# Output projection of a hybrid decoder layer: sixteen token blocks of plain products, or eight block pairs of Strassen's seven products

## The chip, the cores and the metric

One core of one Trainium2 chip runs the whole layer in one launch. The time is device microseconds (us) of that core; smaller is better. Engines: PE = TensorE (matrix products into PSUM), DVE = VectorE, ACT = ScalarE, POOL = GpSimd, SP = SyncE (here it only issues DMAs).

## The reference

Sequence 2048, width 1024, one layer, float32. Only the end is touched by the change:

```python
h = rms_norm(x, ln_g)
proj = h @ w_in                                  # then two head groups
y_mla = mla_group(...) * silu(g_mla)             # 8 heads, causal softmax attention, (2048, 512)
y_hg  = hgrn2_group(...) * silu(g_hg)            # gated linear recurrence, (2048, 512)
x = x + concatenate([y_mla, y_hg], -1) @ w_out   # w_out is (1024, 1024)
return rms_norm(x, final_norm_g)
```

## The kernel before, in words

Float32 operands are split into two fp32r parts, `hi` (a cast, on ACT) and `lo` (the value minus `hi`, on DVE or POOL). A product is three matmuls, hi·hi, hi·lo, lo·hi, all summed in PSUM (`mm3`, L67 to L70).

The program has three stages. Up to about 700 us it does the input projection and the recurrence. Then comes **attention**: 8 heads of 8 steps, 64 steps in all, each of 256 queries. Step n runs stage B of (head, j) together with stage A of the next step. Stage A: scores in three matmuls (L881 to L883), DVE moves them out of PSUM with the running minimum (L886, L890), ACT takes the exponential (L895) into an `sn` row tile (four buffers). Stage B: PE transposes the `sn` tiles (L929), ACT casts the result to `ph` (L932), DVE makes `pl` (L933), PE applies them to the values (L947, L948), POOL scales the gate (L914), and `finish` (L953 to L962) multiplies by the gate on POOL (L960) and stores 64 rows of `y` into `y_d` in DRAM (L962). Between these, pieces of the next head's work are placed (keys, values, queries; POOL makes their `lo` at L814, L829, L842).

The **output projection** stands behind. `load_wout` (L974 to L990) runs at step 60 (`WOUT = 4` steps into the last head): four loads of 1 MB of `w_out` (L979), eight casts of 128x1024 on ACT (L984), eight subtractions (L985, the first on DVE, seven on POOL). The loop of L1040 to L1080 then goes over 16 blocks of 128 tokens: load the block of `y` transposed (L1047), cast on ACT (L1048), `lo` on DVE (L1049), load `x` (L1051); for each of two halves of 512 columns, 8 x 3 matmuls of 128x512 (`mm3`), DVE adds `x` (L1062), ACT squares and sums (L1063); POOL starts the sum (L1066), DVE multiplies by `final_norm_g` (L1067) and ends the sum (L1069), POOL takes the power (L1072), ACT scales one half (L1073), DVE the other (L1074), and SP stores (L1076 to L1079). The last block's second half is cut in two. That is 744 matmuls of 128x512 and 48 of 128x256.

A scheduler sets the order of each engine's instructions from the program; every engine then takes its own in that order and waits at each for what it needs. SP issues all DMAs in one order too. Matmuls of the output projection for early blocks are placed among the last steps of attention, where they fill PE's time.

Of the kernel before, what the change touches and what calls it, by code (L numbers as in the profile page):

```python
# [10 lines left out]
F32 = mybir.dt.float32  # L11
# [5 lines left out]
ALU = mybir.AluOpType  # L17
# [20 lines left out]
WOUT = 4  # L38
# [19 lines left out]
def hybrid_kernel(ctx: ExitStack, tc: tile.TileContext, x, x_t, positions, ln_g, w_in, q_a_norm_g, w_q_b,  # L58
# [719 lines left out]
    def prep(h):  # L778
# [52 lines left out]
        def query(c):  # L831
# [5 lines left out]
            qf = wk.tile([128, 512], F32, tag="qf", bufs=1, name="qf")  # L837
            V.tensor_tensor(qf, p, csT[:, sl], ALU.mult)
            qh = wk.tile([128, 512], F32R, tag="qh", bufs=2, name="qh")
            ql = wk.tile([128, 512], F32R, tag="ql", bufs=2, name="ql")  # L840
# [64 lines left out]
    def stage_b(h, j, ctx_, par):  # L905
# [44 lines left out]
        def finish():  # L950
# [6 lines left out]
            tmp = wk.tile([64, 256], F32, tag="oa", name="oa")  # L957
# [16 lines left out]
    def load_wout():  # L974
        p2r.close()
        wo = p2r.enter_context(tc.tile_pool(name="wo", bufs=1, side="right"))
        for k2 in range(KT // 2):
            wr = wk.tile([128, 2, D], F32, tag="vp", name="vp")
            DMA.dma_start(wr, w_out[k2 * 256:(k2 + 1) * 256, :].rearrange("(k p) n -> p k n", p=128))  # L979
            for j in range(2):  # L980
                k = 2 * k2 + j
                a = wo.tile([128, D], F32R, name=f"wo_hi{k}")
                b = wo.tile([128, D], F32R, name=f"wo_lo{k}")
                A.copy(a, wr[:, j])  # L984
                (V if k == 0 else G).tensor_tensor(b, wr[:, j], f32(a), ALU.subtract)  # L985
                w_hi.append(a)
                w_lo.append(b)
# [48 lines left out]


    p3 = ExitStack()
    op = p3.enter_context(tc.tile_pool(name="op", bufs=2, side="right"))
    fng = wk.tile([128, D], F32, tag="ks", bufs=1, name="ks")  # L1040
    DMA.dma_start(fng, final_norm_g.rearrange("(o n) -> o n", o=1).broadcast_to([128, D]))
    for b in range(NBLK):
        c, r0 = b // 4, b * 128
        t0 = (b % 4) * 128
        yh = op.tile([128, KT, 128], F32R, tag="yh", name="yh")
        yl = op.tile([128, KT, 128], F32R, tag="yl", name="yl")
        DMA.dma_start(f32(yl), y_d[c][:, t0:t0 + 128].rearrange("(k p) t -> p k t", p=128))  # L1047
        A.copy(yh, f32(yl))  # L1048
        V.tensor_tensor(yl, f32(yl), f32(yh), ALU.subtract)  # L1049
        xt = wk.tile([128, D], F32, tag="vp", name="vp")  # L1050
        DMA.dma_start(xt, x[r0:r0 + 128, :])  # L1051
        last = b == NBLK - 1
        cuts = (0, 512, 768, 1024) if last else (0, 512, 1024)
        ssq = small.tile([128, 3], F32, tag="ssq3", name="ssq3")
        ot = wk2.tile([128, D], F32, tag="sn", bufs=4, name="sn")
        r = None
        for i in range(len(cuts) - 1):
# [53 lines left out]
```

## Time and profile before

| | us |
|---|---|
| median of 3 runs (1418.79, 1419.00, 1421.24) | 1419.0 |
| the profiled execution's own time | 1418.87 |
| its span, first to last instruction | 1417.1 |
| PE busy | 1387.7 |
| DVE busy | 958.6 |
| ACT busy | 881.2 |
| POOL busy | 464.8 |

The span is divided among engines in the page's first part; an engine can be busy beside others, so the shares don't add up. The chain of waits follows back from the last instruction what released each instruction, so its shares do add up. A window gives each engine's busy time in a stretch.

### The profile page before, as it was taken

How to read it: one execution, taken by the hardware profiler on the slowest of the kernel's cores; microseconds unless marked ns; L12 is line 12 of the kernel's file. 1: busy time of each engine (PE TensorE's matmuls, PEld its weight loads, DVE VectorE, ACT ScalarE, POOL GpSimd, SP SyncE). 2: the span in 40 equal slices, each digit the busy share in tenths (PEclk: the TensorE clock that was granted, in tenths of full speed). 3: DMA queues.
4: the chain of work that ended last, by engine and by line, in shares of the span. 5: the costliest groups of instructions: out<-in, count | busy, mean ns of one | idle time of the engine just before them, and what ended most of it. 6: DMA issues, size and time to landing. Idle time of an engine off the chain costs nothing.

```text
span 1417.1 us, 25792 instructions
## 1 busy us (share of the span) xinstructions
PE 1387.7 (98%) x9258; PEld 1263.5 (89%) x9258; DVE 958.6 (68%) x2425; ACT 881.2 (62%) x1796; POOL 464.8 (33%) x635
## 2 busy tenths in 40 slices
PE   8999999999999999999899999999999999999998
PEld 7899879989899988998889898999999998888887
DVE  6547855595845845658388889898889889743333
ACT  6565575456862647355388778778777878732232
POOL 3123613083121622237252425233342525411010
PEclk9999999999999999999989999999999999999999
DMA  7211211215411112111630000100010103244442
GB/s 230 75 48 46 75 53 31 67 42 172 138 46 34 54 52 82 38 42 44 194 73 18 19 22 13 24 13 22 13 26 11 25 22 107 74 144 143 134 148 104
DMA packets 100576, 96.30 MB, mean 68 GB/s; under 512 B 31200, under 2 KB 88800, under 8 KB 100320
## 3 DMA queue, kind: packets, MB, share of 16 engines
q1 hardware_dynamic: 100448, 94.65, 22.7%
q8 instruction: 73, 1.20, 0.4%
q14 instruction: 55, 0.45, 0.1%
HBM read 68.41 MB, written 25.17 MB: 66 GB/s over the span
## 4 chain that ended last, share of the span: by engine, by line
PE 85%; DVE 5%; POOL 3%; ACT 2%; issue 2%; DMA 2%; SPq 0%; POOLq 0%; DVEq 0%; ACTq 0%
PE ps_mm L68 14%; PE ps_mm L69 14%; PE ps_mm L70 14%; PE ps_tp L929 8%; PE ps_a L948 5%; PE ps_a L947 4%; PE ps_mm L881 4%; PE ps_mm L883 4%; PE ps_mm L882 4%; PE ps_b L70 2%; PE ps_b L68 2%; PE ps_b L69 2%; PE ps_a L486 2%; PE ps_b L486 1%; POOL dd L468 1%
## 5 line engine op out<-in xcount | busy, mean ns | idle before, releaser
L68 PE MATMUL ps_mm<-w,hh 128*128 128x256 f32 (+3 forms) x896 | 268.3, 299 | 0.0
L69 PE MATMUL ps_mm<-w,hh 128*128 128x256 f32 (+3 forms) x896 | 263.9, 295 | 0.0
L70 PE MATMUL ps_mm<-w,hl 128*128 128x256 f32 (+3 forms) x896 | 263.0, 294 | 0.0
L933 DVE TENSOR_TENSOR pl<-ps_tp,ph 128x512 fp32r<-128x512 f32 (+1 forms) x288 | 184.6, 655 | 33.3 <-ACT ph L932 32.6
L932 ACT CAST ph<-ps_tp 128x512 fp32r<-128x512 f32 (+1 forms) x288 | 154.4, 565 | 60.2 <-PE ps_tp L929 46.7
L68 PEld LDWEIGHTS ps_mm<-w,hh 128*128 128x128 f32 x896 | 170.1, 190 | 0.7
L69 PEld LDWEIGHTS ps_mm<-w,hh 128*128 128x128 f32 x896 | 169.8, 189 | 0.4
L70 PEld LDWEIGHTS ps_mm<-w,hl 128*128 128x128 f32 x896 | 169.3, 189 | 0.1
L929 PE MATMUL ps_tp<-ident,sn 128*128 128x128 f32 x1088 | 167.9, 274 | 0.8 <-ACT sn L895 0.8
L895 ACT ACTIVATE sn<-sn,mx 128x128 f32<-128x128 f32 (+15 forms) x128 | 154.6, 1208 | 21.2 <-DVE mx L890 20.8
L947 PE MATMUL ps_a<-ph,vp 128*128 128x256 f32 x576 | 155.5, 290 | 0.0
L948 PE MATMUL ps_a<-pl,vp 128*128 128x256 f32 x576 | 147.1, 288 | 0.2 <-DVE pl L933 0.2
L468 POOL TENSOR_TENSOR dd<-G 128x512 f32<-128x512 f32 x80 | 92.8, 1164 | 142.9 <-DVE qd L481 106.9
L929 PEld LDWEIGHTS ps_tp<-ident,sn 128*128 128x128 f32 x1088 | 126.8, 140 | 8.8 <-ACT sn L895 1.3
L881 PE MATMUL ps_mm<-k_hi,qh 128*128 128x512 f32 (+3 forms) x320 | 130.8, 409 | 0.5 <-DVE mx L890 0.2
L886 DVE TENSOR_SCALAR_CACHE_REDUCE sn<-ps_mm,mx 128x512 f32<-128x512 f32 (+3 forms) x192 | 111.5, 581 | 10.9 <-PE ps_mm L883 8.8
L883 PE MATMUL ps_mm<-k_hi,ql 128*128 128x512 f32 (+3 forms) x320 | 116.5, 364 | 1.4 <-DVE ql L842 1.4
L882 PE MATMUL ps_mm<-k_lo,qh 128*128 128x512 f32 (+3 forms) x320 | 116.1, 363 | 0.0
L914 POOL TENSOR_SCALAR gp<-gate,ri 128x64 f32<-128x64 f32 x128 | 56.7, 445 | 180.9 <-DVE ri L897 159.7
L230 DVE SCALAR_TENSOR_TENSOR w<-wr,lng,w 128x256 fp32r<-128x256 f32 (+3 forms) x168 | 89.3, 574 | 39.4 <-ACT w L229 39.4
L948 PEld LDWEIGHTS ps_a<-pl,vp 128*128 128x128 f32 x576 | 109.0, 189 | 6.0 <-DVE pl L933 1.2
L947 PEld LDWEIGHTS ps_a<-ph,vp 128*128 128x128 f32 x576 | 108.9, 189 | 5.8 <-ACT ph L932 0.6
(275 smaller groups left out, 3348.5 us busy)
## 6 DMA issues: line engine op xcount, KB each, us to landing
wr<-in_w_in SPq DMA_DIRECT2D x68, 256.0 KB
yl<-y_d SPq DMA_DIRECT2D x16, 512.0 KB
vp<-in_x SPq DMA_DIRECT2D x16, 512.0 KB
out<-sn SPq DMA_DIRECT2D x15, 512.0 KB
xt<-in_x SPq DMA_DIRECT2D x8, 512.0 KB
xs<-in_x_t SPq DMA_DIRECT2D x8, 512.0 KB
y_d<-yt SPq DMA_DIRECT2D x16, 256.0 KB
gate<-gate_d SPq DMA_DIRECT2D x8, 512.0 KB
```

The lines of the kernel that those rows point to most:

```text
L68: PE.matmul(ps, l_hi, r_hi, start=start, stop=False)
L69: PE.matmul(ps, l_hi, r_lo, start=False, stop=False)
L70: PE.matmul(ps, l_lo, r_hi, start=False, stop=stop)
L881: PE.matmul(p[:, :w], qh[:, qs], kh[:, ks], start=True, stop=False)
L882: PE.matmul(p[:, :w], qh[:, qs], kl[:, ks], start=False, stop=False)
L883: PE.matmul(p[:, :w], ql[:, qs], kh[:, ks], start=False, stop=True)
L895: A.activation(sn[:, :nk], sn[:, :nk], AF.Exp, bias=mx[:, kc:kc + 1], scale=-1.0, accum_out=rs)
L929: PE.transpose(tp[:, o:o + 128], prow[i][:, (kb + u) * 128:(kb + u + 1) * 128], ident)
L932: A.copy(ph[:, :w], tp[:, :w])
L933: V.tensor_tensor(pl[:, :w], tp[:, :w], f32(ph[:, :w]), ALU.subtract)
L947: PE.matmul(dst, vv, ph[:, rng], start=st_, stop=False)
L948: PE.matmul(dst, vv, pl[:, rng], start=False, stop=en)
```

## The change

The output projection is computed by the Winograd form of Strassen's scheme. For a pair of 128-token blocks, `y` is split into four quadrants (token block by half of the 1024 inner values: a11, a12, a21, a22) and `w_out` into four of 512x512 (b11, b12, b21, b22). Seven products of 128x512 with an inner length of 512 take the place of eight, on sums of quadrants: s1 = a21 + a22, s2 = s1 - a11, s3 = a11 - a21, s4 = a12 - s2, and t1 = b12 - b11, t2 = b22 - t1, t3 = b22 - b12, t4 = b21 - t2 (the sign of t4 as the code has it). Partial sums stay in PSUM: bank a takes a11·b11, is copied to bank b by ACT (L1205), then also takes a12·b21; b takes s2·t2, is copied to bank c (L1210), then takes s3·t3 and a22·t4; c takes s4·b22; e takes s1·t1. Each product is 12 matmuls (`product`, L1166 to L1168). The last pair's seventh product is cut in two halves of 256 columns. Two more matmuls of 128x512 (L1154) start banks b and c.

The weight sums are made by `wout_sums` (L991 to L1023) in eight items (128 rows of each half of `w_out`, 256 columns of each half): two loads (L1004), four POOL subtractions of 128x256 (L1010 to L1013), two ACT casts (L1018, 128x1024 and 128x768), two POOL `lo` subtractions of the same shapes (L1019), four stores (L1021) into `w_d` in DRAM. That is 14 MB stored, and read back as seven sets of 2 MB (`wload`, L989): b11, t1, t2, b21, t3 from step 59 on (`WOUT = 3`), b22 and t4 in the last step, when pool `big` is closed. The written plan gives item i the steps 8 + 6i and on.

`pair_operands` loads a pair's `y` (L1064, 1 MB) and `x` (L1070, 1 MB), makes the sums s1 to s4 on DVE (L1082, 128x512) and splits seven operands (ACT cast L1074, DVE L1075, 128x512 each). `after` adds `x` (L1172, six of 128x512 a pair) and ends as before (L1181 to L1201).

```diff
-WOUT = 4
+WOUT = 3
...
-    def load_wout():
...
+    ORDER = (("a11", "b11", "a"), ("s1", "t1", "e"), ("s2", "t2", "b"), ("a12", "b21", "a"),
+             ("s3", "t3", "b"), ("s4", "b22", "c"), ("a22", "t4", "b"))
...
+        def sums():
+            w, t = o["w"], four()
+            o["t"] = t
+            G.tensor_tensor(t[:, 0], w[:, 1], w[:, 0], ALU.subtract)
+            G.tensor_tensor(t[:, 1], w[:, 3], t[:, 0], ALU.subtract)
+            G.tensor_tensor(w[:, 1], w[:, 3], w[:, 1], ALU.subtract)
+            G.tensor_tensor(t[:, 2], w[:, 2], t[:, 1], ALU.subtract)
+
+        def split(src, s0, n):
+            hi = four(F32R)
+            lo = src[:, :n].bitcast(F32R)
+            A.copy(hi[:, :n], src[:, :n])
+            G.tensor_tensor(lo, src[:, :n], f32(hi[:, :n]), ALU.subtract)
+            for i, t in enumerate((hi[:, :n], lo)):
+                DMA.dma_start(f32(w_d[:, s0:s0 + n, i, kk, ns]), f32(t))
...
+    for i in range(8):
+        for k, f in enumerate(wout_sums(i // 2, i % 2)):
+            pieces[8 + 6 * i + k] = [f]
...
+            side = [open_wout, early("b11")]
+        elif first > 0 and n < len(seq) - 1:
+            side = side + [early(name) for name in {1: ("t1",), 2: ("t2", "b21"), 3: ("t3",)}[first]]
+        elif n == len(seq) - 1:
+            side = [open_late] + pair_operands(0)[:4] + [late("b22"), late("t4")]
...
-    for b in range(NBLK):
...
+        def residual():
+            xt = wk2.tile([128, 2, D], F32, tag="sn", bufs=4, name="sn")
...
+            DMA.dma_start(xt, x[r0:r0 + 256, :].rearrange("(r p) n -> p r n", p=128))
...
+        def after(i):
+            if i == 0:
+                A.copy(acc["b"], acc["a"])
+            elif i == 1:
+                add(0, H1, acc["e"])
+                add(1, H1, acc["e"])
+            elif i == 2:
+                A.copy(acc["c"], acc["b"])
+            elif i == 3:
+                add(0, H0, acc["a"])
+                done(0, H0, True)
...
+    run(pair_operands(0)[4:])
+    for b in range(NBLK // 2):
+        merge(pair_products(b), pair_operands(b + 1) if b + 1 < NBLK // 2 else [])
```

Where the scheduler puts these can't be read from the diff. Three places matter. In the rows below, a row is one instruction (x2, x3: so many alike), and the brackets name the engines and DMA queues it waits for; line numbers of the kernel before are lower by two in attention.

**POOL in the first steps of attention, before** (`gp` is the gate, `oa` the finished values, `ql` the query's `lo`):

```order
L914 TENSOR_SCALAR gp<-gate,ri 128x64 [waits DMAHW4_49,DMAHW3_49,DMAHW5_49,DMAHW1_49,DMAHW6_49,DMAHW0_49,DVE_49]
L914 TENSOR_SCALAR gp<-gate,ri 128x64 [waits DVE_49] x3
L814 TENSOR_TENSOR vp<-vs,vp 128x4x64 [waits Activation_49]
L960 TENSOR_TENSOR oa<-oa,og 64x256 [waits DVE_49]
L842 TENSOR_TENSOR ql<-qf,qh 128x512 [waits PE_49,Activation_49]
L914 TENSOR_SCALAR gp<-gate,ri 128x64 [waits DVE_49,PE_49]
L814 TENSOR_TENSOR vp<-vs,vp 128x4x64 [waits Activation_49]
L960 TENSOR_TENSOR oa<-oa,og 64x256 [waits DVE_49]
```

**The same place in the change:**

```order
L1010 TENSOR_TENSOR ss<-ss 128x256 [waits DMAHW6_49]
L1011 TENSOR_TENSOR ss<-ss 128x256 [waits DMAHW7_49,Pool_49]
L1012 TENSOR_TENSOR ss<-ss 128x256
L916 TENSOR_SCALAR gp<-gate,ri 128x64 [waits DMAHW1_49,DVE_49]
L1013 TENSOR_TENSOR ss<-ss 128x256 [waits Pool_49]
L916 TENSOR_SCALAR gp<-gate,ri 128x64 [waits DVE_49] x2
L1019 TENSOR_TENSOR ss<-ss 128x1024 [waits Activation_49,Pool_49]
L916 TENSOR_SCALAR gp<-gate,ri 128x64 [waits DVE_49]
L816 TENSOR_TENSOR vp<-vs,vp 128x4x64 [waits Activation_49]
L962 TENSOR_TENSOR oa<-oa,og 64x256 [waits DVE_49]
```

The eight items' 48 POOL instructions (`ss`) stand in the rows that belong to steps 0 to 14, between the gates and the `lo` of the next head, and not at the steps of the written plan.

**DVE near the end of attention, before** (`pl` belongs to the last steps' stage B, L1062 is the first block's adding of `x`):

```order
L933 TENSOR_TENSOR pl<-ps_tp,ph 128x512 [waits PE_49,Activation_49] x2
L1062 TENSOR_TENSOR vp<-ps_mm,vp 128x512 [waits DMAHW4_49,DMAHW6_49,DMAHW2_49,DMAHW7_49,PE_49,Pool_49]
L933 TENSOR_TENSOR pl<-ps_tp,ph 128x512 [waits DVE_49,Activation_49]
L1067 TENSOR_TENSOR vp<-vp,ks 128x512 [waits Activation_49]
L933 TENSOR_TENSOR pl<-ps_tp,ph 128x384 [waits Activation_49]
L933 TENSOR_TENSOR pl<-ps_tp,ph 128x512 [waits Activation_49] x2
L1062 TENSOR_TENSOR vp<-ps_mm,vp 128x512 [waits PE_49]
L1069 SCALAR_TENSOR_TENSOR rx<-ssq_15799,rx 128x1 [waits Activation_49,Pool_49]
```

**DVE in the last step, in the change:**

```order
L935 TENSOR_TENSOR pl<-ps_tp,ph 128x512 [waits Activation_49]
L1172 TENSOR_TENSOR sn<-ps_mm,sn 128x512 [waits DMAHW1_49]
L1172 TENSOR_TENSOR sn<-ps_mm,sn 128x512
L935 TENSOR_TENSOR pl<-ps_tp,ph 128x512 [waits PE_49,Activation_49] x2
L935 TENSOR_TENSOR pl<-ps_tp,ph 128x512 [waits Activation_49] x2
L935 TENSOR_TENSOR pl<-ps_tp,ph 128x384 [waits Activation_49]
L1075 TENSOR_TENSOR pl<-vp,ph 128x512 [waits PE_49,Activation_49] x2
L961 TENSOR_TENSOR oa<-ps_a,oa 64x256 [waits DMAHW5_49,Activation_49]
L1172 TENSOR_TENSOR sn<-ps_mm,sn 128x512 [waits PE_49] x2
L1189 TENSOR_TENSOR sn<-sn,fng 128x512 [waits Activation_49]
L1172 TENSOR_TENSOR sn<-ps_tp,sn 128x512 [waits PE_49]
L1082 TENSOR_TENSOR ss<-vp 128x512 [waits DMAHW6_49]
```

The first two additions of `x` (L1172, out of bank e) now stand between two `pl` of the last step and wait for the DMA of pair 0's `x`; the sums and splits for pair 1 (from L1082) come in a row behind.

**SP in the last step, in the change** (`y_d` is stored by `finish`; L1070 loads `x` for pairs 0 to 3, the last L1064 loads `y` for pair 1):

```order
L964 DMA y_d_71<-oa 64x256 [waits DMAHW5_49,Pool_49]
L989 DMA b22s<-wd 128x4096 [waits DMAHW6_49,PE_49,Activation_49]
L989 DMA t4s<-wd 128x4096 [waits DMAHW7_49,Activation_49]
L964 DMA y_d_71<-oa 64x256 [waits DMAHW0_49,Pool_49]
L1070 DMA sn<-in_x 128x2x1024 [waits DMAHW1_49,PE_49,Activation_49]
L1070 DMA sn<-in_x 128x2x1024 [waits DMAHW2_49,PE_49,Activation_49]
L964 DMA y_d_72<-oa 64x256 [waits DMAHW3_49,Pool_49]
L1070 DMA sn<-in_x 128x2x1024 [waits DMAHW4_49,PE_49,Activation_49]
L1070 DMA sn<-in_x 128x2x1024 [waits DMAHW5_49,PE_49,Activation_49]
L1064 DMA vp<-y_d_69 128x8x256 [waits DMAHW6_49,PE_49]
```

Pair 0's `x` is issued behind the reloads of b22 and t4, and waits for PE, that is for the last transposes out of the `sn` tile that it takes over; pair 1's `y` is issued behind four loads of `x` and waits for the last application of the values on PE (`vp`).

## Rows read from the trace of the kernel before

**Rows 1.** The page's first part: busy us (share of span), instructions of each engine.

```profile
PE 1387.7 (98%) x9258; PEld 1263.5 (89%) x9258; DVE 958.6 (68%) x2425; ACT 881.2 (62%) x1796; POOL 464.8 (33%) x635
```

**Rows 2.** The page's fourth part: shares by engine of the chain that ended last.

```profile
PE 85%; DVE 5%; POOL 3%; ACT 2%; issue 2%; DMA 2%; SPq 0%; POOLq 0%; DVEq 0%; ACTq 0%
```

**Rows 3.** Windows: busy us of PE, PEld, DVE, ACT, POOL (instructions), clock, DMA share, GB/s.

```profile
720.00:845.00 125.00, 124.76 (x851) 113.69 (x850) 108.37 (x347) 99.85 (x210) 45.02 (x69) 1.00 0.08 19
1185.00:1206.00 21.00, 19.91 (x124) 16.52 (x123) 20.07 (x59) 20.28 (x35) 13.75 (x12) 1.00 0.48 149
1224.00:1411.00 187.00, 186.91 (x899) 157.23 (x896) 73.68 (x118) 59.73 (x117) 22.48 (x37) 1.00 0.39 128
```

**Rows 4.** Timeline of PE, first output-projection matmuls: start us, us, instruction.

```profile
1224.10 0.48 PE L68 MATMUL ps_mm<-wo_hi,yh 128*128 128x512 f32 x1
1224.64 0.40 PE L70 MATMUL ps_mm<-wo_hi,yl 128*128 128x512 f32 x1
1227.86 0.40 PE L69 MATMUL ps_mm<-wo_lo,yh 128*128 128x512 f32 x1
```

**Rows 5.** Timelines of PE and SP at the end of the span.

```profile
1409.31 0.28 PE L68 MATMUL ps_b<-wo_hi,yh 128*128 128x256 f32 x1
1410.63 0.28 PE L70 MATMUL ps_b<-wo_hi,yl 128*128 128x256 f32 x1
1413.95 0.38 SPq L1076 DMA_DIRECT2D out<-sn  x1
```

**Rows 6.** Groups of instructions by line and shape: busy us, mean ns, idle before.

```profile
L932 ACT CAST ph<-ps_tp 128x512 fp32r<-128x512 f32 x224 | 125.9, 589 | 56.2 <-PE ps_tp L929 43.3 <-PE ps_a L947 10.3
L1048 ACT CAST yh<-yl 128x1024 fp32r<-128x1024 f32 x16 | 16.8, 1050 | 10.4 <-DMA yl<-y_d 10.3
L1049 DVE TENSOR_TENSOR yl<-yl,yh 128x1024 fp32r<-128x1024 f32 x16 | 20.1, 1254 | 23.6 <-ACT yh L1048 23.6
L1062 DVE TENSOR_TENSOR vp<-ps_mm,vp 128x512 f32<-128x512 f32 x21 | 14.5, 688 | 24.4 <-PE ps_mm L70 23.1 <-DMA vp<-in_x 1.2
L1063 ACT ACTIVATE sn<-vp 128x512 f32<-128x512 f32 x31 | 19.6, 632 | 89.7 <-DVE vp L1062 85.7 <-PE ps_tp L929 4.0
L814 POOL TENSOR_TENSOR vp<-vs,vp 128x256 fp32r<-128x256 f32 x24 | 17.4, 737 | 21.8 <-ACT vp L813 21.8
L985 POOL TENSOR_TENSOR wo_lo<-vp,wo_hi 128x1024 fp32r<-128x1024 f32 x7 | 16.8, 2414 | 5.8 <-ACT wo_hi L984 5.8
```

**Rows 7.** Timeline of ACT in attention, around 1185 us.

```profile
1185.43 2.00 ACT L984 CAST wo_hi<-vp 128x1024 fp32r<-128x1024 f32 x2
1190.25 2.24 ACT L1048 CAST yh<-yl 128x1024 fp32r<-128x1024 f32 x2
```

**Rows 8.** Timeline of PE just behind it.

```profile
1193.68 1.20 PE L929 MATMUL ps_tp<-ident,sn 128*128 128x128 f32 x9 [0.76 <-ACT sn L895]
```

**Rows 9.** Timelines of SP and ACT: one weight load issued, and its first use.

```profile
1202.25 0.38 SPq L979 DMA_DIRECT2D vp<-in_w_out  x1
1207.88 2.00 ACT L984 CAST wo_hi<-vp 128x1024 fp32r<-128x1024 f32 x2
```

**Rows 10.** Timeline of POOL beside VectorE, around 1192 us.

```profile
1191.70 2.05 POOL L960 TENSOR_TENSOR oa<-oa,og 64x256 f32<-64x256 f32 x1
1193.36 1.47 DVE L1049 TENSOR_TENSOR yl<-yl,yh 128x1024 fp32r<-128x1024 f32 x1
```

**Rows 11.** Windows: a stretch with much DMA traffic.

```profile
1186.00:1190.00 4.00, 3.89 (x22) 3.03 (x21) 3.75 (x12) 3.95 (x8) 2.49 (x2) 1.00 0.95 260
```

**Rows 12.** Timeline of PE: an idle time ahead of attention.

```profile
703.95 0.55 PE L68 MATMUL ps_mm<-wv_hi,c_hi 128*128 128x256 f32 x1 [2.28 <-ACT gt L365]
```

**Rows 13.** Windows around it.

```profile
700.00:704.00 4.00, 1.72 (x12) 1.36 (x10) 1.12 (x3) 1.90 (x4) 0.27 (x1) 1.00 1.04 256
704.00:716.00 12.00, 7.75 (x22) 5.66 (x23) 10.84 (x19) 10.01 (x19) 10.53 (x10) 0.50 0.97 252
716.00:720.00 4.00, 4.00 (x23) 3.43 (x23) 2.89 (x13) 2.61 (x8) 2.56 (x4) 0.79 0.99 163
```

More of the change, by code (lines that the diff above doesn't have):

```diff
@@ L956, in finish @@
                 A.copy(gs[:, i * 128:(i + 1) * 128], gT[i * 64:(i + 1) * 64, 0:128])
[L957 removed]
+            tmp = wk.tile([64, 256], F32, tag="oa", bufs=3, name="oa")
             A.copy(tmp, av[64:128])
@@ new lines, in hybrid_kernel, with wload, wout_sums, four @@
+    wset = {}
+    ys = [{} for _ in range(NBLK // 2)]
+    o_pools = {}
+    SETS = ("b11", "t3", "b21", "b22", "t1", "t2", "t4")
+    w_d = dram.tile([128, 7, 2, 4, 512], F32R, name="wd")
+    def wload(pool, name):
+        wset[name] = pool.tile([128, 2, 4, 512], F32R, name=name + "s")
+        DMA.dma_start(f32(wset[name]), f32(w_d[:, SETS.index(name)]))
+    def wout_sums(kk, ch):
+        ns = slice(ch * 256, ch * 256 + 256)
+        o = {}
+        def four(dtype=F32):
+            return fin.tile([128, 4, 256], dtype, tag="ss", bufs=3, name="ss")
+        def load():
+            o["w"] = four()
+            for g in range(2):
+                r0 = g * 512 + kk * 128
+                DMA.dma_start(o["w"][:, 2 * g:2 * g + 2],
+                              w_out[r0:r0 + 128, :].rearrange("p (c n) -> p c n", c=2)[:, :, ns])
+        def sums():
[12 more added lines that the diff above has]
+                DMA.dma_start(f32(w_d[:, s0:s0 + n, i, kk, ns]), f32(t))
+        return [load, sums, lambda: split(o["w"], 0, 4), lambda: split(o["t"], 4, 3)]
@@ new lines, in late, with operand @@
+    def late(name):
+        return lambda: wload(o_pools["ln"], name)
+    ln = ExitStack()
+    def operand(name):
+        if name in ("a11", "s1"):
+            if "ks" not in o_pools:
+                o_pools["ks"] = wk.tile([128, 2, 2, 4, 128], F32R, tag="ks", bufs=1, name="ks")
+            t = o_pools["ks"][:, ("a11", "s1").index(name)]
+        elif name == "s2":
+            t = o_pools["ln"].tile([128, 2, 4, 128], F32R, tag=name, name=name)
+        elif name in ("s3", "s4"):
+            t = wk2.tile([128, 2, 4, 128], F32R, tag="gate", name="gate")
+        else:
+            return (wk2.tile([128, 4, 128], F32R, tag="ph", bufs=3, name="ph"),
+                    wk2.tile([128, 4, 128], F32R, tag="pl", bufs=3, name="pl"))
+        return t[:, 0], t[:, 1]
```

170 lines of the change are left out of this document (110 added, 60 removed).

## The prediction, made before the changed kernel had run

> **What bounds the kernel now.** I read the page's busy times first, to find the fullest engine: PE is busy 1387.7 of 1417.1 us, 98%, and no other engine is over 68% [rows 1]. The chain of waits then says whether that fullness sets the end: PE holds 85% of it, DVE 5% [rows 2]. Shares are averages, so I read windows by stage. In the output projection PE is busy 186.91 of 187 us while DVE has 73.7 and ACT 59.7 [rows 3]: it is bound by PE alone, and work taken from PE comes off the time if the others keep up. In attention PE is busy too (124.76 of 125), but there DVE has 108.4, ACT 99.9 and POOL 45.0 [rows 3]: PE's lead is thin, and what is added on ACT or POOL must be checked. The profiled execution took 1418.87 us, 1.8 over its span and 0.1 under the median of the runs, so the sum below is made against 1418.9. About 0.2% (2.8 us) is what a measurement of this kernel can tell from no change.
>
> **1. Products: -21.7.** Fourteen matmuls of 128x512 start in 1227.86 - 1224.64 = 3.22 us, 0.23 each [rows 4]; eleven of 128x256 in 1410.63 - 1409.31 = 1.32, 0.12 each [rows 5]. Before: 744 of the wide and 48 of the narrow. Now: 8 pairs x 7 x 12 = 672, of which the last 12 are cut into 24 halves, so 660 wide, 24 narrow, and two wide ones that start banks b and c. Saved: 84 x 0.23 + 24 x 0.12 - 2 x 0.23 = 21.7. PE is gapless there, so all of it comes off.
>
> **2. `load_wout` goes: -1.** Its casts lie on ACT in pairs of 2.00 us, and two of L1048 in 2.24 [rows 7]. Behind these PE waits 0.76 for the exponential [rows 8]; the stretch loses 1.1 of 21 [rows 3]. Pair 0's splits come into the same last steps, so I take 1 between 0 and -1.1, nearer the row's loss, as they are single casts of about 0.59 [rows 6].
>
> **3. Weight sums in steps 0 to 14: +2.** The order puts all eight items there. Each costs POOL four subtractions of 0.74, one of 2.41, and one of three quarters of that, 1.81 [rows 6]: 7.2, times eight 57.5. POOL goes from 45.0 of 125 to about 102, 82%. ACT gets 1.05 + 0.79 per item, 14.7 in all, and goes from 99.9 to 114.6, 92%; DVE stays at 108.4. PE's queue waits in order for POOL's `ql` and `gp` and ACT's `ph`. Lower end 0, as this stretch loses 0.24 now. Upper end: where ACT is at 97% and DVE at 96%, PE lost 1.1 of 21 [rows 3], over 125 us that is 6.5. ACT stays below that, so 2. The 18 MB that the items load and store in this stretch meet a DMA share of 0.08 [rows 3]; the stores wait for POOL on SP, and behind them stand the next heads' loads and `y`'s stores, which have steps of room.
>
> The Trainium skill (GPSIMD Engine Reference, section 4.1, Engine selection) speaks against the place: elementwise work with two inputs belongs on VectorE, GpSimd being about twice as slow. The trace agrees on speed, 2.41 us against 1.25 for the same 128x1024 [rows 6]. But by the rule 30 us would go to a DVE that has 16.6 us free in 125 [rows 3], so this term would be about +13 and not +2; idle time on POOL is what counts here.
>
> **4. Pair 0's `x` comes late: +4.** The two additions out of bank e stand on DVE between `pl`'s of the last step, so those `pl`'s and PE's applications behind them wait for this load. It can be issued only after the last transposes of the step before, which free its `sn` tile. From there to the matmul that needs the first held `pl` the order has 24 transposes of 0.13 [rows 8] and about 24 narrow matmuls of 0.12, 6.0 us. A load of 1 MB took 1207.88 - 1202.25 = 5.6 us from issue to first use [rows 9]; two additions and one `pl` of 0.69 each make 7.7. Wait at least 7.7 - 6.0 = 1.7. At most: if t4's 2 MB, issued just ahead, are still to come, 8 us more at 260 GB/s [rows 11], so 9.7. The 14 MB of reloads take 54 us at that rate, about the length from step 59 to there, so part is in flight: 4.
>
> **5. Pair 1's operands come late: +4.** Its `y` is issued after attention's last matmul on the values, behind four loads of `x`, two of which are issued only some 2 us earlier. From there PE has 46 wide matmuls of pair 0, 10.6 us. Landing at 5.6 with a free queue, or 5.6 + 2 x 3.85 - 2 = 11.3 behind two loads; the cast takes 0.59 and three DVE steps 2.1 [rows 6]: PE waits about 2.5, and 1.5 more as s1's `lo` stands seven DVE steps on while PE has 3.2 us of a11·b11. Ends: 0 and 9 (all four loads ahead).
>
> **6. The clock falls after such waits: +3.** Ahead of attention PE waited 2.28 us [rows 12]; the granted clock was 1.00 up to there, then 0.50 for 12 us, and mixed (0.79) in the next 4 us [rows 13]: the lower level, 1.2 of 2.4 GHz. PE waited on within those 12 us. A PE that is busy again loses half of the low time, so a wait of 4 us or so may cost 0 to 6 more. Two such waits: ends 0 and 12, taken 3, as a slower PE also lets DVE and DMA catch up and pays back part of items 4 and 5.
>
> **7. Less to fill the last steps with: +1.** By the order, 85 wide matmuls of early blocks lay between attention's last ones before; now pair 0's first three products do, 36, so PE is more exposed to ACT and DVE. By the rate of 1.1 in 21 [rows 3] over some 20 us, +1, between 0 and 2.
>
> **Nothing:** a pair has 84 matmuls, 19.3 us. DVE has 6 additions, 2 multiplications, 4 sums, 7 `lo` at 0.69 and 2 scalings, 15 us; ACT two copies, seven casts, four squares, two scalings, 10 us: covered by PE, and if that cover went each would show in full. The tail behind PE's last matmul has the same steps. Sum: -21.7 - 1 + 2 + 4 + 4 + 3 + 1 = -8.7, so **1410.2 us**.
>
> **The rivals.**
> - *Everything lands in time.* Items 4, 5 and 6 go. For it: DMA has been busy only 0.39 in the projection [rows 3]. Against it: the order ties both loads to late releases. 1418.9 - 21.7 - 1 + 2 + 1 = 1399.2.
> - *POOL and ACT crowd attention.* Item 3 at its upper end and some more, 1416. For it: POOL's L960 took 2.05 us beside DVE's L1049, which took 1.47 [rows 10], against a mean of 1.25 [rows 6]: the two slow each other. Against: DVE's operations in this stretch read PSUM with one input. The Trainium skill (same page, section 8, Key points) has such contention for two SBUF inputs on VectorE; by that, the trace agrees.
> - *The hand-over between pairs stalls (slower).* Between a22·t4 and s2·t2 of the next pair stand 13 matmuls, 2.97 us; in that time DVE adds (0.69), ACT squares (0.63 and 0.19 for the sum) and copies a to b. No row has a copy from PSUM to PSUM; the nearest is the cast out of PSUM, 0.59 [rows 6]. That leaves 0.65 with hand-overs counted at 0.2. If copy or queue take 1.7 us longer, PE waits about 1.1 in each of 8 pairs, which eats the 8.7; at 2 us each it is 1410.2 + 16 = 1426.
> - *The weights come late.* That the items do not spread as planned helps the reload; but if 14 MB move at 200 GB/s, b22 and t4 end 16 us later than at 260, of which PE has some 6 in hand: +10, 1420.
>
> **How the numbers follow.** Forecast 0.54 (own range 1404 to 1416), all in time 0.20, crowded 0.11, hand-over 0.08, weights late 0.07. Faster by over 2.8: 0.53 + 0.20 + 0.07 of crowded + 0.01 = 0.81. Same: 0.01 + 0.04 + 0.02 + 0.02 = 0.09. Slower: 0.06 + 0.04 = 0.10. The range reaches down past the second case, to 1397, and up past the crowded one, to 1417; above lie most of the last two, below the rest of the second.
>
> **What would show it.** PE's pace stays at 0.23 and its busy time falls by about 22. One idle time of 2 us or more on PE in the last step, released by DVE's `pl` behind L1172, with that waiting for the DMA of `x`; a second ahead of pair 1's first product, released by DVE or ACT behind L1064's load; a clock of 0.50 for some us after either. POOL near 80% in the first 130 us of attention with few PE waits. From pair 2 on no PE idle time. If PE waits ahead of each s2·t2, the third rival holds; if it waits for b22 or t4 themselves, the fourth; if attention as a whole got longer by over 6 us, the second.

## The result, and the profile of the changed kernel

The changed kernel took **1428.39 us** (median of 9 runs, 1426.62 to 1436.06) where the kernel before took 1419.70 (9 runs, 1418.22 to 1424.07): ratio 1.0069, interval [1.0050, 1.0088]. It is slower by some 9 us; the forecast was 1410.2, with 1417 as its upper end.

The page of the profiled execution, first and fourth part, to set beside [rows 1, 2]:

```profile
PE 1382.8 (97%) x9152; PEld 1248.5 (87%) x9152; DVE 1004.0 (70%) x2512; ACT 910.9 (64%) x1860; POOL 508.9 (36%) x676
...
PE 76%; DVE 8%; DMA 5%; ACT 5%; issue 3%; POOL 3%; SPq 0%; POOLq 0%; ACTq 0%; DVEq 0%
```

PE has less to do and holds a smaller share of the chain; DVE, ACT and DMA hold more. This execution took 1434.3 us, 6 over the median. To find where time goes I follow one instruction through both traces: the last `ps_a<-ph,vp` matmul of a step. First the kernel before, at steps 0, 15, 56 and 63, with a store of stage 1 (L347) as the mark ahead of attention:

```profile
722.76 0.22 PE L947 MATMUL ps_a<-ph,vp 128*128 128x128 f32 x1
853.65 0.23 PE L947 MATMUL ps_a<-ph,vp 128*128 128x128 f32 x1
1179.64 0.22 PE L947 MATMUL ps_a<-ph,vp 128*128 128x128 f32 x1
1260.13 0.22 PE L947 MATMUL ps_a<-ph,vp 128*128 128x128 f32 x1
...
679.37 0.32 SPq L347 DMA_DIRECT2D latkv_d<-lo  x1
```

The same places in the changed kernel:

```profile
733.87 0.22 PE L949 MATMUL ps_a<-ph,vp 128*128 128x128 f32 x1
875.96 0.23 PE L949 MATMUL ps_a<-ph,vp 128*128 128x128 f32 x1
1202.90 0.22 PE L949 MATMUL ps_a<-ph,vp 128*128 128x128 f32 x1
1272.26 0.23 PE L949 MATMUL ps_a<-ph,vp 128*128 128x128 f32 x1
...
682.30 0.32 SPq L347 DMA_DIRECT2D latkv_d<-lo  x1
```

Stage 1, which the change does not touch, ended 2.93 us later in this execution; in the other traces of this case its mark stands between 0.3 earlier and 2.2 later than in the kernel before, so I take this as variation. Less that, PE is late by 8.2 us at step 0, by 19.4 at step 15, by 20.3 at step 56 and by 9.2 at the end of attention. The span is 15.4 longer; less 2.93 that is 12.5, some 3 more than the medians differ by (8.7), so that much of what follows belongs to this execution. Three things happened: **8 us were lost as attention began, 11 more in steps 0 to 15, and the projection gave back 8 where 22 were expected.** "Delay" below is this number. It is good to a few us as attention starts (the mark does not catch all of stage 1's variation), better for growth from step to step.

**As attention begins.** PE's rows with a wait of over 1.9 us, then SP's rows at that place and the two issues of L791 by themselves (shortest, median and longest in ns), in the changed kernel; last, the same loads in the kernel before:

```profile
707.98 0.39 PE L68 MATMUL ps_mm<-wv_hi,c_hi 128*128 128x256 f32 x1 [2.57 <-ACT gt L365]
712.02 0.80 PE L68 MATMUL ps_b<-c_hi,wk_hi 128*128 128x512 f32 x1 [3.06 <-ACT ks L828]
721.82 0.47 PE L883 MATMUL ps_mm<-k_hi,qh 128*128 128x128 f32 x1 [8.15 <-ACT qh L843]
731.83 0.33 PE L955 MATMUL ps_b<-ident,gp 128*128 128x128 f32 x1 [1.94 <-POOL gp L916]
...
706.58 8.24 SPq L791 DMA_DIRECT2D gate<-gate_d  x2
714.91 1.64 SPq L366 DMA_DIRECT2D gate_d<-gt  x1
L791 SPq DMA_DIRECT2D gate<-gate_d x2: 359/3506/6652, 706.6 to 708.2; - x2
...
710.83 1.56 SPq L789 DMA_DIRECT2D gate<-gate_d  x2
```

Before, the longest wait here was 2.28 [rows 12]. ACT's rows say why the cast `qh` is late:

```profile
719.36 0.86 ACT L812 COPY vs<-ps_mm 128x384 f32<-128x384 f32 x2 [2.44 <-DMA gate_d<-gt]
720.11 1.14 ACT L830 CAST k_hi<-ks 64x512 fp32r<-64x512 f32 x2
721.15 0.62 ACT L843 CAST qh<-qf 128x512 fp32r<-128x512 f32 x1
```

`vs` waits for the store of a stage-1 tile (`gt`): the change gives the pools of attention another order, and `vs`, `qf`, `qh` and `ql` move into pool `big`, which now lies over the stage-1 pool that holds `gt`. As the program places the tiles, `vs` itself lies over another tile of that pool, so the wait is for the pool and not for `gt`'s own bytes. The store stands on SP behind two loads of the gate (L791), at which SP stood 8.24 us: the second was issued at 708.2, and its issue took 6.65 us. No view shows a wait for PE there, and why the issue took so long is open; before, both loads stood behind that store and took 1.56. ACT takes its queue in order, so `qh` waits behind `vs`. The last wait, for `gp`, is another matter: on POOL the gate stands among the first item's subtractions (L1010 to L1013).

**Steps 0 to 15.** The window of [rows 3] in the changed kernel; then the same work, from the mark of step 0 to that of step 15, before and in the change; then the change's longest wait of PE between these marks (us in total, times, longest):

```profile
720.00:845.00 125.00, 115.96 (x733) 101.00 (x733) 97.12 (x309) 100.21 (x205) 97.44 (x113) 0.97 0.55 169
...
722.80:853.70 130.90, 130.90 (x902) 119.76 (x901) 114.22 (x359) 104.83 (x219) 46.60 (x70) 1.00 0.08 18
733.90:876.00 142.10, 136.64 (x903) 120.93 (x902) 116.57 (x361) 118.23 (x236) 98.15 (x115) 1.00 0.46 143
...
PE ps_a L949 <- ACT ph L934: 2.7, 3, 1.5
```

The same 902 matmuls took 11.2 us more. POOL rose by 51.6 us of work and ACT by 13.4 (reckoned: 57.5 and 14.7), DVE by 2.4. Of the 11.2, 5.5 is idle time of PE; the other 5.7 stands in its busy time, where starts lie further apart but still within the modelled length of a row. Before, PE has no idle time here. The longest wait, row by row:

```profile
801.47 0.74 POOL L1010 TENSOR_TENSOR ss<-ss 128x256 f32<-128x256 f32 x1 [2.31 <-DMA wd<-ss]
804.00 1.04 ACT L1018 CAST ss<-ss 128x1024 fp32r<-128x1024 f32 x1 [1.75 <-POOL ss L1012]
804.95 0.85 ACT L934 CAST ph<-ps_tp 128x384 fp32r<-128x384 f32 x2
805.48 0.38 PE L949 MATMUL ps_a<-ph,vp 128*128 128x256 f32 x1 [1.47 <-ACT ph L934]
```

ACT stood idle 1.75 us at an item's cast, for POOL's sums, which had waited for the store that frees their tile. The two `ph` stood behind that cast, though their transposes had ended at 803.3, and PE waited for them. So an engine can hold PE up here while it is itself idle.

**The projection.** Waits from 1180 us on:

```profile
PE ps_a L950 <- DVE pl L935: 2.0, 2, 1.0
PE ps_mm L1166 <- ACT ps_mm L1205: 1.9, 1, 1.9
PE ps_tp L931 <- ACT sn L897: 1.1, 1, 1.1
PE ps_mm L1168 <- DVE ks L1075: 0.6, 1, 0.6
PE ps_mm L1166 <- DVE sn L1172: 0.5, 1, 0.5
```

Then the spacing of the wide matmuls, first in the kernel before, then in the changed one (18 apart):

```profile
1299.82 0.39 PE L69 MATMUL ps_b<-wo_lo,yh 128*128 128x512 f32 x1
1303.90 0.39 PE L69 MATMUL ps_mm<-wo_lo,yh 128*128 128x512 f32 x1
```

```profile
1299.75 0.39 PE L1167 MATMUL ps_mm<-t3s,gate 128*128 128x512 f32 x1
1303.95 0.39 PE L1167 MATMUL ps_tp<-b22s,gate 128*128 128x512 f32 x1
```

4.08 / 18 = 0.2267 before, 4.20 / 18 = 0.2333 after: the same shape, the same granted clock of 1.00, and 3% slower. With each matmul from step 56 on counted at the median spacing of its shape in the kernel before, PE's work fell from 227.3 to 205.9 us, 21.4 less, which is what the forecast has. But the starts spread over 17.0 us more than that, where it was 3.7 before: 4.4 more in attention's last steps, 5.3 in gaps among products, 3.7 of slower spacing. With the 0.3 by which the tail behind PE grew, 20.3 - 21.4 + 13.3 + 0.3 = 12.5.

### The profile page after: what moved, and what is told of

Same layout as the page of the kernel before. It is cut to its first block, busy times and chain, and to the rows that moved or that the text cites. A ratio compares the mean times of both kernels' runs of the same rounds, so it can differ in the third digit from the quotient of the medians.

```text
span 1432.5 us, 25853 instructions
## 1 busy us (share of the span) xinstructions
PE 1382.8 (97%) x9152; PEld 1248.5 (87%) x9152; DVE 1004.0 (70%) x2512; ACT 910.9 (64%) x1860; POOL 508.9 (36%) x676
## 4 chain that ended last, share of the span: by engine, by line
PE 76%; DVE 8%; DMA 5%; ACT 5%; issue 3%; POOL 3%; SPq 0%; POOLq 0%; ACTq 0%; DVEq 0%
PE ps_mm L68 11%; PE ps_mm L69 11%; PE ps_mm L70 11%; PE ps_tp L931 7%; PE ps_a L950 4%; PE ps_a L949 4%; PE ps_mm L883 4%; PE ps_mm L885 4%; PE ps_mm L884 4%; PE ps_mm L1166 3%; PE ps_mm L1167 3%; PE ps_mm L1168 3%; PE ps_b L486 1%; PE ps_a L486 1%; POOL dd L468 1%
## 5 line engine op out<-in xcount | busy, mean ns | idle before, releaser
L931 PEld LDWEIGHTS ps_tp<-ident,sn 128*128 128x128 f32 x1088 | 126.5, 141 | 12.5 <-ACT sn L897 2.9
```

Source lines behind the costliest of these rows:

```text
L931: PE.transpose(tp[:, o:o + 128], prow[i][:, (kb + u) * 128:(kb + u + 1) * 128], ident)
```

## The experiments

Delays are against the trace of the kernel before, in us; time is the median, with the number of runs. The kernel before, run beside them, had 1420.4 to 1421.0.

```
kernel                       delay at step  0     6    15    56    63   time (runs)
changed kernel                            8.2  12.8  19.4  20.3   9.2   1428.4 (9)
e0 before, places of the change           4.9   6.5   6.1   6.1   6.1   1427.1 (4)
e1 gate apart, items bunched              1.8  10.0  16.2  17.2   5.9   1429.3 (4)
e2 items at their steps                   4.1   6.0   7.4  15.0   3.5   1429.4 (4)
e3 both                                   2.1   3.7   5.8  10.8  -0.6   1420.7 (10)
e4 e3, first query aside                 -1.2   0.7   2.9   7.9  -3.7   1421.1 (10)
a1 e4 without GpSimd's arithmetic        -4.2  -2.2   0.8  12.7   1.4   1424.0 (1)
a2 e4 without the casts                  -3.7  -1.7   1.0   7.3  -4.1   1420.2 (1)
a3 e4 with loads and stores only          2.5   4.5   4.9   6.9  -4.8   1417.4 (1)
e5 e4 with a pad of 32 bytes             -0.5   1.4   3.6   8.7  -2.8   1416.4 (9)
e6 e5, hand-over turned round            -0.3   1.6   4.0   8.8  -3.0   1416.8 (10)
e7 e6 with a pad in stage 1               1.7   3.5   6.0  11.1  -0.4   1418.7 (10)
f1 e7 with small pieces                  -1.5   0.3   5.3  12.7   1.3   1422.1 (10)
g1 changed kernel with the pad            6.7  13.9  20.5  21.2   9.4   1428.1 (9)
g2 e5, weight sets moved too             -3.5  -1.7   0.8   5.9  -4.9   1417.1 (1)
g3 e4, weight sets moved alone            2.0   3.9   6.3  11.6  -0.1   1418.9 (1)
g4 changed kernel, loads and stores only  6.1   8.5   8.5   9.6  -1.8   1420.8 (1)
```

### The places (e0)

```diff
-    big = p2.enter_context(tc.tile_pool(name="big", bufs=1, side="left"))
...
+    fin = p2.enter_context(tc.tile_pool(name="fin", bufs=1, side="left"))
+    fin.tile([128, 4096], F32, name="pad")
+    p2k = ExitStack()
+    big = p2k.enter_context(tc.tile_pool(name="big", bufs=1, side="left"))
...
-            qh = wk.tile([128, 512], F32R, tag="qh", bufs=2, name="qh")
+            qh = big.tile([128, 512], F32R, tag="qh", bufs=2, name="qh")
```

`vs`, `qf` and `ql` move in the same way as `qh`.

> The kernel before with nothing of the change but the places of its tiles: pools in the order wk, wk2, fin (one unused tile of 16 KB), big, with vs, qf, qh and ql in big, oa with three buffers. The projection and the weights are as before. If the 10 us that the change lost at the start of attention come from the new places (the gate's tile over operands that PE still reads, so that its load blocks SP ahead of the last gate store, and vs over tiles that wait for that store): 8 to 11 us slower than before, 1428 to 1430, with a wait of about 8 us on PE for ACT's qh near 714. If they come from the weight sums' loads and stores beside it: within 2 us of before, 1418 to 1421.

1427.05 us (1425.32 to 1427.81), ratio 1.0049 [1.0032, 1.0066]. Products, weights and items are those of the kernel before; only places differ, and PE's wait is there:

```profile
720.12 0.47 PE L884 MATMUL ps_mm<-k_hi,qh 128*128 128x128 f32 x1 [8.29 <-ACT qh L844]
```

The delay is 6.1 from step 15 to step 63 and nothing is given back. So the places alone cost about 7 us, a little under the 8 to 11 expected, and the rival of no cost is out. What they do not show is the reason in the brackets, that the gate's load waits for PE.

### Gate apart, items at their steps, both (e1 to e3)

```diff
+    gtp = p2.enter_context(tc.tile_pool(name="gtp", bufs=2, side="left"))   # e1, e3: the gate's tiles
...
+            # e2, e3: a write to the item's tile that needs the step's softmax sum
+            G.tensor_scalar(out=t[:, 2, 0:1], in0=live["ri"], scalar1=1.0, scalar2=None, op0=ALU.mult)
```

e1 holds only the first item's load, e3 holds each load as well.

> The change with the gate's tiles in a pool of their own above fin, and the first item's loads and the load of final_norm_g held back by a small POOL write from a step's ri, so that nothing stands on SP ahead of the last gate store; the weight items stay in the first 14 steps. By the theory of the places: the wait of 8 us on PE goes, 8 to 10 us faster than the change, 1418 to 1421. By the rival that the traffic of the items makes the wait: no more than 2 us faster, 1426 to 1429.

1429.32 (1426.51 to 1433.07): missed. The wait on `qh` fell to 5.79, and then the bunched items took more than that back, 8 us by step 6 and 14 by step 15.

> The change with each item's sums held to the step of the written plan (8 + 6i and on) by a POOL write of 128x1 from that step's ri; the places are the change's. If POOL and ACT crowd steps 0 to 14, the second loss of 10 us between steps 0 and 14 goes: 8 to 10 us faster, 1418 to 1421, and the start of attention still loses about 10. If the items cost the same wherever they stand, the loss is spread over 50 steps: 1426 to 1430.

1429.36 (1426.33 to 1430.26): the rival's range. Spread out, the items cost about 1 us each wherever they stand (7.4 to 15.0 between steps 15 and 56). POOL's `gp` is waited for 3.5 us in all.

> The change with both edits: gate's tiles in their own pool, and loads and sums of each item held to the planned step. If the two losses are separate, they add up: 16 to 20 us faster than the change, 1409 to 1412, which is 8 to 11 faster than before. If one hides behind the other, about 1418.

1420.68 (1418.22 to 1423.84), ratio 1.0004 [0.9991, 1.0017]: 8 us better than either alone, 10 worse than the sum expected, and 2.7 off the other branch (1418). The items still cost 5 from step 15 to step 56, and `qh` is still waited for 5.60.

### The first query aside (e4)

```diff
-    big = p2k.enter_context(tc.tile_pool(name="big", bufs=1, side="left"))
+    big = p2k.enter_context(tc.tile_pool(name="big", bufs=1, side="left", reuse_waits="tile"))
...
+            if h == 0 and c == 0:
+                qf, qh, ql = (fin.tile([128, 512], t, tag="ss", bufs=3, name="ss") for t in (F32, F32R, F32R))
```

> The run before this one (gate tiles in a pool of their own, weight items held at their steps) gave 1420.7 us against 1420.4 for the kernel before; its trace still had a TensorE wait of 5.6 us at the start of attention, on head 0's first query (ScalarE's cast qh). This kernel adds: the big pool is reused tile by tile, and head 0's first query takes its three tiles (qf, qh, ql) from fin's tag ss, which lies over nothing that stage 1 still reads. Theory 'places': the start then runs as in the kernel before, the 2 to 4 us of delay in steps 0 to 3 go, the rest stays: 1416 to 1418 us, no TensorE wait over 3 us between 715 and 730. Rival 'the first steps are short of engine time whatever the places': the wait on qh goes to another tile, time 1419 to 1422.

By the trace the theory: the start is that of the kernel before, delay 0.7 at step 6, PE's longest wait 2.7 us. By the time the rival: 1421.07 (1419.56 to 1423.73), with none of the 3 us that the trace gained on e3. The profiled run of e3 was one of its slowest (1423.51), that of e4 its fastest (1419.56), so part of that gain is chance; how much is open.

### What in an item costs (a1, a2, a3, f1, g4)

```diff
-            G.tensor_tensor(t[:, 0], w[:, 1], w[:, 0], ALU.subtract)      # a1, a3, g4: the four sums and the two lo
-            A.copy(hi[:, :n], src[:, :n])                                 # a2, a3, g4
+            G.tensor_tensor(hi[:, :n], src[:, :n], src[:, :n], ALU.subtract)   # a2, in the place of the lo
...
+            def piece(q):                                                 # f1: 256 columns at a time
+                A.copy(hi[:, q], o[src][:, q])
+                G.tensor_tensor(lo, o[src][:, q], f32(hi[:, q]), ALU.subtract)
```

> The first kernel of this call without GpSimd's arithmetic in the weight items (sums and remainders are left out, so the second factors are not formed and the output is not the reference's); the casts on ScalarE, the loads and the stores stay in number and size. An item costs TensorE 0.8 to 1 us between steps 8 and 56. Theory 'GpSimd': the 2.05 us subtractions stand ahead of the gate products and remainders that attention waits for; without them the delay from step 6 to step 56 falls from about 7 us to under 2. Rival 'ScalarE': the casts of 0.95 us stand ahead of ph and the exponentials; then the delay stays at 5 to 7.

> The first kernel of this call without ScalarE's casts in the weight items (GpSimd writes the high part's tile in the place of the cast, so the stored factors and the output are not the reference's); GpSimd's instructions, loads and stores stay in number and size. Theory 'GpSimd': the delay from step 6 to step 56 stays at 5 to 7 us. Rival 'ScalarE': it falls to under 2. If both this and the kernel without GpSimd's sums keep about half, each engine carries a part.

In a2 the high part is zero and the whole sum stands in the low part. From step 6 to step 56 the delay grew by 14.9 us in a1 and by 9.0 in a2, against 7.2 with everything in place. Neither expectation holds, and taking work away made it worse. The scheduler writes the order of all engines anew for each kernel. Counted as the fewest of the 3600 attention matmuls in the traces that have to be moved to turn one order into the other, e4 differs from the kernel before by 617, and from e4 a1 differs by 478 and a2 by 459. So these two do not split an item's price between the engines; that stays open.

> The kernel with the first query set aside and the items at their steps, with neither GpSimd's arithmetic nor ScalarE's casts in the weight items: only the loads and the stores are left, the loaded rows are stored as they are, so the second factors are not formed and the output is not the reference's. Without GpSimd's arithmetic alone the delay from step 6 to step 56 was 14.9 us, without the casts alone 9.0, with both in place 7.2: neither engine's work carries it alone. The orders of the attention matmuls differ between those kernels (the scheduler writes the order anew). Theory 'an item's work of either engine costs, through the order the scheduler then writes': without both the delay from step 6 to step 56 is under 2 us. Rival 'the loads and stores' (DMA traffic of 65 GB/s where the kernel before had 22): it stays at 5 or more.

Growth 2.4 from step 6 to step 56 (384 matmuls moved against e4): close to the theory's 2, far from the rival's 5.

> The kernel before this one in the call, with the casts and remainders of the weight items cut into 256-wide pieces (56 of each in place of 16), two to a step. Theory 'long items stand in the way': a cast of 0.95 us and a subtraction of 2.1 us no longer hold up ph and the gate products; the delay from step 6 to step 56 falls from 7 to 3 us, 3 to 4 us less. Rival 'the order that the scheduler writes decides': the delay changes by some us in either direction, with no relation to the length of the pieces.

1422.05 (1419.24 to 1424.66), some 3 us worse than e7; growth 12.4 against 7.6. More and shorter instructions did not help. The rival fits, which is no proof of it.

> The changed kernel without GpSimd's arithmetic and ScalarE's casts in the weight items: the loaded rows are stored as they are, so the second factors are not formed and the output is not the reference's; pools and places are the change's, and the order of the attention matmuls is but for 166 of 3577 the same. The delay of TensorE against the kernel before stands at 8 us at step 0 and 19 at step 15 in the changed kernel. Theory 'the items' work in steps 0 to 14': it now grows by 0 to 3 us from step 0 to step 15, and the time is 8 to 11 us less than 1428.4. Rival 'the loads and stores or the places': it still grows by 8 or more.

This one is made on the changed kernel, whose order it nearly keeps (146 of the 3600 matmuls moved). The window and the only listed wait from step 0 to 860 us:

```profile
720.00:845.00 125.00, 123.51 (x805) 111.39 (x806) 104.42 (x341) 96.96 (x204) 46.23 (x70) 0.97 0.56 177
...
PE ps_mm L68 <- DVE sn L888: 0.2, 1, 0.2
```

DMA moves as much as in the changed kernel (177 GB/s against 169), and PE is back at 123.5 of 125: the delay grows by 2.4 from step 0 to 15, not by 11.2. So about 9 us in these steps are the items' arithmetic on POOL and ACT, not their traffic by itself. At step 0 the delay is 6.1 where it was 8.2: the wait for `gp` is gone. How the 9 divide between POOL and ACT is not shown. One run took 1420.81, 7.6 less (8 to 11 expected). The Trainium skill (SBUF — State Buffer, section "SBUF: two separate sides") has it that DMA and engines reach SBUF by separate ports and can't contend; this window agrees.

### The spacing of the products (e5, e7, g2, g3, g1)

```diff
+    pad = p2.enter_context(tc.tile_pool(name="pad", bufs=1, side="left"))    # e5, g1, g2: ahead of wk
+    pad.tile([128, 8], F32, name="pad")
+    pad1 ...                                                                 # e7: the same ahead of stage 1's pools
+    padr ... side="right"                                                    # g2, g3: the same ahead of the weight sets
```

> The same kernel with one unused tile of 32 bytes a partition ahead of the pool wk, so that all tiles on the left side of SBUF stand 32 bytes further on. Question: why do the projection's 512-wide matmuls follow each other at 0.2333 us in the changed kernel and at 0.2267 in the kernel before. Theory 'alignment': in the changed kernel the stationary operands start at multiples of 64 bytes and the moving ones 32 bytes off, before both were 32 off; with the pad both are: pace 0.2267 to 0.2303, 2 to 4 us less than the kernel without the pad. Rival 'not the alignment' (which side of SBUF, or the other engines' traffic): pace stays at 0.2333, same time.

1416.35 (1413.56 to 1422.54), a ratio of 0.9978 [0.9960, 0.9995] to the kernel before; against e4, whose order of attention's matmuls is the same, the median is 4.7 less and the mean 3.9. Eleven spacings of one product:

```profile
1319.75 0.39 PE L1179 MATMUL ps_mm<-b21s,ph 128*128 128x512 f32 x1
1322.27 0.39 PE L1181 MATMUL ps_mm<-b21s,pl 128*128 128x512 f32 x1
```

2.52 / 11 = 0.2291.

> The kernel before this one in the call, with a second unused tile of 32 bytes ahead of the pools of stage 1, so that the operands of its input products (stationary hh and hl, moving w) stand 32 bytes off multiples of 64, where they stood at multiples of 64. About 740 of its matmuls run 512 wide at 0.231 us. Theory 'alignment holds there too': pace 0.2267, 740 x 0.0045 = 3.3 us less. Rival 'only a mix of the two alignments, or another property of the projection, slows': no change of pace, same time within 1 us.

The spacing in stage 1 stayed at 0.231, the time at 1418.70 (1415.99 to 1419.55), 1.9 more than e6: nothing gained. There both operands stand on the same side and moved together, from multiples of 64 to 32 off.

> The kernel with the first pad of 32 bytes (stationary operands 32 bytes off multiples of 64, pace 0.2267), and a second pad on the right side ahead of the weight sets, so that these moving operands, which stood 32 off, start at multiples of 64 (s2, which is stationary and lies on that side, too). Theory 'the stationary operand decides': pace stays at 0.2267, but for the product with s2, which goes to 0.2333. Rival 'the two have to stand alike': pace 0.2333, but for the product with s2.

> The same second pad without the first: stationary operands and weight sets all start at multiples of 64. Theory 'the stationary operand decides': pace 0.2333 for all sets. Rival 'the two have to stand alike': 0.2267 for all sets. Anything between, such as the 0.231 of stage 1, where both stood at multiples of 64, would speak for a third property.

The same product in g2, then in g3:

```profile
1319.25 0.39 PE L1181 MATMUL ps_mm<-b21s,ph 128*128 128x512 f32 x1
1321.82 0.40 PE L1183 MATMUL ps_mm<-b21s,pl 128*128 128x512 f32 x1
```

```profile
1322.40 0.39 PE L1179 MATMUL ps_mm<-b21s,ph 128*128 128x512 f32 x1
1324.92 0.39 PE L1181 MATMUL ps_mm<-b21s,pl 128*128 128x512 f32 x1
```

g2: 2.57 / 11 = 0.2336; g3: 0.2291. With the two operands alike, both at a multiple of 64 bytes (g3) or both 32 off (e5), matmuls follow at 0.229; with one of each (changed kernel, g2) at 0.2335. The product with s2, whose two operands lie on the same side and stand alike in all four, kept 0.228 in e5, g2 and g3 and 0.230 in the changed kernel. "The two have to stand alike" holds, the stationary operand alone does not decide, and e7 fits. Alike there are still three values, 0.2267 in the kernel before, 0.229 and stage 1's 0.231; why is open.

> The changed kernel with nothing but an unused tile of 32 bytes a partition ahead of the pool wk; TensorE's order of work is the same. Theory 'the place of the stationary operands': the pace goes from 0.2333 to 0.2267 as it did in the kernel with the other mendings, 672 x 0.0067 = 4.5 us less: 1424 us against 1428.4. Rival 'worth less here, since other waits take up the time': 1427 to 1429.

The spacing fell to 0.229 here too, and from step 63 to the end this trace lost 0.9 us where the changed kernel's lost 3.3. The time, 1428.12 (1424.88 to 1431.31), ratio 1.0053 [1.0038, 1.0067], can't be told from 1428.39. By these traces the spacing is worth 2.4 us, by 672 x 0.0042 it is 2.8; g1's times neither show nor exclude that. (e5's trace is 4.0 shorter than e4's from step 63 on, but 1.7 of that is the clock of the next section.)

### The hand-over to the last pair (e6)

In the changed kernel, around PE's wait of 1.9 us:

```profile
1407.35 0.69 DVE L1172 TENSOR_TENSOR sn<-ps_mm,sn 128x512 f32<-128x512 f32 x1 [2.17 <-PE ps_mm L1168]
1408.13 0.63 ACT L1181 ACTIVATE junk<-sn 128x512 bf16<-128x512 f32 x1 [2.99 <-DVE sn L1172]
1408.76 0.58 ACT L1205 COPY ps_mm<-ps_mm 128x512 f32<-128x512 f32 x1
1409.39 0.50 PE L1166 MATMUL ps_mm<-t2s,s 128*128 128x512 f32 x1 [1.85 <-ACT ps_mm L1205]
...
1408.00:1416.00 8.00, 6.61 (x22) 5.25 (x23) 0.95 (x3) 2.50 (x5) 0.55 (x1) 0.79 0.16 66
```

Add, square, copy, matmul, one behind the other, and a granted clock of 0.79 in the 8 us behind it: there eight matmuls in a row start 0.43 apart, at the lower of the clock's two levels (3.4 us of it), which costs 1.7 us. That does not always follow: the same wait of 1.85 us stands in thirteen traces, and the clock fell behind it in five (the change, e3, e4, a2, g1) and stayed at 1.00 in eight, as here in e5, whose wait ends at 1393.10:

```profile
1391.00:1399.00 8.00, 6.14 (x28) 4.86 (x27) 1.69 (x4) 2.50 (x5) 0.55 (x1) 1.00 0.19 74
```

```diff
             if i == 0:
                 A.copy(acc["b"], acc["a"])
+                if b:
+                    ys[b - 1]["end"]()
...
-                done(1, H0, False)
-                finish(1, H1, H0)
+                o["end"] = lambda: (done(1, H0, False), finish(1, H1, H0))
```

> The kernel with the pad of 32 bytes (1416.35 us) and one move: the squares and the finish of a pair's last quarter are written behind the next pair's copy of bank a, so that ScalarE makes that copy first. Theory 'the hand-over': TensorE's wait of 1.85 us at the start of the last pair's second factor set and the lower clock granted behind it go: 2 to 3.5 us less, 1413 to 1414.5. Rival 'that stretch is not the end's': the wait goes, but the last add, norm and store end when they did: within 1 us of 1416.4.

1416.80 (1414.41 to 1418.36), ratio 0.9973 [0.9961, 0.9985]: the rival by the time, neither by the trace. The longest wait for this copy fell to 1.2, but there are two now, 1.9 in sum, so the hand-over was not removed, and the clock had stayed up in e5 already.

e5 and e6 beat both kernels, by some 3 to 4 us against the one before and some 12 against the change.

## Why the prediction was wrong

**The products were right.** 21.4 us of PE's work went (term 1: 21.7). Its assumption was not: "all of it comes off" at 0.23 each. The forecast read spacing off the rows as a property of the shape; it is one of the places too. 0.2333 against 0.2267 over 672 matmuls is 4.5 us (3.7 by the count above).

**Term 3 (weight sums, +2, ends 0 and 6.5) is the term that failed.** It was 11.2 us in steps 0 to 15, about 9 of it from POOL's and ACT's arithmetic (g4), and the 1.9 of `gp` at step 0 beside it. The work added to the engines was near what was reckoned (51.6 and 13.4 us), but the size was taken by share of busy time, from a stretch in which ACT and DVE were full. PE's queue in attention waits in order for `ph`, which now stood behind casts of 1.05 us that themselves waited for POOL, and for `gp`, which stood among subtractions of 0.74 to 2.4 us; this shows with ACT busy 118 of 142 us and POOL 98. So the second rival was the true course of attention, at one and a half times its price (1416 is 5.8 over the forecast, so 7.8 for this term). Its argument, that POOL and DVE slow each other, was a small part at most: DVE's work grew by 2.4 us.

**A term was missing.** The working counts every instruction and no place. That tiles of attention now lie over stage-1 pools still in use cost some 6 of the 8.2 us at step 0 (6.1 in g4, without the items' arithmetic); e0 gives 7 for it alone, in time. The lines that reorder the pools stood in the change and got no price.

**Terms 4 and 5 were too large, and the end lost as much in other places.** Pair 0's `x` and pair 1's operands, reckoned at 4 each:

```profile
1266.67 1.29 DVE L1172 TENSOR_TENSOR sn<-ps_mm,sn 128x512 f32<-128x512 f32 x2 [0.79 <-DMA sn<-in_x]
1268.62 0.39 PE L950 MATMUL ps_a<-pl,vp 128*128 128x256 f32 x1 [1.02 <-DVE pl L935]
1287.34 0.51 PE L1168 MATMUL ps_mm<-t1s,ks 128*128 128x512 f32 x1 [0.61 <-DVE ks L1075]
...
1210.00:1230.00 20.00, 17.66 (x107) 14.40 (x106) 18.76 (x58) 14.15 (x29) 6.23 (x9) 1.00 1.02 421
```

1.0 and 0.6 us, at the places and by the releasers that were named. The reloads ran at 421 GB/s where 260 was the row at hand [rows 11], so no weight set was late: the first rival was right about the reloads, and the fourth is out. The clock stayed at 1.00 behind these two; it fell at another place, behind the last pair's hand-over, for 1.7 us and not in every trace (term 6: 3). Term 7 (+1) came out at 2.1 in its two longest waits, 1.05 at 1215.7 and 1.02 at 1219.5. Term 2 was not measured by itself. Terms 2 and 4 to 7 add up to 11 and the end lost 13.3 more than before; that the sums are near is luck, since most of it is spacing, the hand-over and short gaps, which none of these terms had.

**The third rival** held in one pair of eight: the copy out of PSUM took 0.58 as its nearest row said, but with the square ahead of it PE waited 1.9. Turning it round (e6) split the wait between two pairs and did not shorten the kernel.

Together, by the trace: 8.2 at the start, 12.1 in attention, 13.6 of losses more at the end with the tail, against 21.4 saved: 12.5, some 3 more than the medians show. Against the forecast, the start of attention and its steps (the missing term and term 3) are off by 18 of these us, the end by 2.6.

## What to carry to other kernels

Work put on an idle engine is not free when a full engine waits in order for that engine's small results: price it by what stands behind each long instruction and by what that instruction itself waits for, not by busy shares. When a change reorders pools, list which tiles of the last stage lie under the first tiles of the next, and who still reads them; that is a term of the sum like any other.

## What the runs showed of the hardware

- The spacing of 512-wide fp32r matmuls depended on where the operands start: 0.229 us with stationary and moving alike modulo 64 bytes, 0.2335 with one of them 32 bytes off.
- Behind one and the same wait of PE of 1.85 us the granted clock fell to its lower level for 3.4 us in five traces and stayed at 1.00 in eight.
- Reloads from DRAM ran at 421 GB/s for 20 us, beside a PE that was busy 17.66 of 20.
- 177 GB/s of traffic in attention, without the items' arithmetic, left PE 123.5 us busy in 125.
